# SSD products of a group in one cluster over two banks; transposes of values and x written pairwise

## The chip, the cores and the metric

The kernel runs on one core of a Trainium2 chip. The metric is device microseconds of one execution, the median of several runs; lower is better. A profile is one execution recorded instruction by instruction on the same kind of chip. Engines: PE multiplies matrices, DVE, ACT and POOL work on elements, SP issues most of the transfers.

## The reference

Two residual layers over 272 tokens (16 learned meta tokens and 256 real ones) of width 2048, each a mixer, a projection back and a layer norm. The first mixes with gated linear attention (GLA, 4 heads) and stick-breaking attention (8 heads). The second is a Mamba-2 SSD mixer: 64 heads of width 64 in 8 groups, which share B and C of state size 128 within a group. Without the chunking, what the second layer computes per head is

```python
x, B, C, dt = split(silu(causal_conv(h @ w_in)))
L[t, s]  = exp(sum of dt*a over s < r <= t) for s <= t, else 0
y[t]     = sum_s  (C[t] . B[s]) * L[t, s] * dt[s] * x[s]  +  d_skip * x[t]
out      = rms_norm_per_group(y * silu(z)) @ w_out
```

and GLA per head is, for the output dimension v, `o[t] = sum_s (q[t] * exp(G[t] - G[s])) . k[s] * v[s]` over s <= t, followed by an RMS norm and a SiLU gate.

## The kernel before

All weights stream through as units of 1 MB (`L0`, `L1` list them in order). A unit's weights are split into a high and a low part of reduced-precision fp32 (`whi` by ACT on L146, `wlo` by DVE or POOL on L147, five buffers each), and each product of it is done as three: high by high, high by low, low by high (L165 to L167 for the projections in, L453 to L455 for the second layer's projection out). An "in" unit is 48 such products of 256 to 274 columns, an "out1" unit 24 of 512 columns. They are called the main products here. Projections accumulate in the PSUM tiles `pj` (four banks).

Between them stands the work of the mixers, in full fp32: PE takes every such product in two passes, except transposes, which take one. These write to the PSUM tiles `po` (two banks) or to the two banks `z0`, `z1` (`zbank()` hands them out in turn). A run of fp32 instructions between two main products is called a set. The mixers are generators; `tick()` advances each by one step after a fixed number of main products. A scheduler then orders every engine's instructions by a simulation of its own, so that a piece can be issued later than it is written, and pieces written together can be drawn apart.

The places that the change touches:

- `to_tokens` turns a value unit of GLA or stick-breaking (128 values by 272 tokens) to tokens on partitions: a copy to `vraw` by ACT, then three transposes (L539 twice, L540 for the last 16 tokens), then four copies out of the bank. GLA has four value units a head, so four such sets.
- `mix_gla` multiplies scores by values: for each of four j a bank, three products in parts like the main ones, then the fp32 products of the second token block (L646) and of the last 16 tokens (L647, 16 rows deep).
- Second layer, per group g: units B, C, x0 to x3, z0 to z3, then, from group 2, four out1 units of group g-2. `x_path(g, j)` takes x units two at a time: SiLU (DVE, three ACT steps, a POOL product on L955), then four transposes of 128 columns (L1053) and two of 16 (L1054), then DVE products by dt into `xd` (L1062) and `xd2` (L1064).
- `decay1` makes the matrices `M` of the eight heads (DVE L992 and L993, exp by ACT), the small `mt` for the last 16 tokens, multiplies B by C (L1006 to L1008, in a z bank), masks the result on POOL, and multiplies M (L1019, two of four on POOL from group 2) and mt (L1022) by it.
- `mix_ssd` waits for all of that, then, for each j of four, a bank with two heads side by side in 64 columns each of the PE: first 128 tokens (L1100, 256 columns), second block (L1102, 144 columns), last 16 tokens (L1104, 16 rows deep, 16 columns). After each j: DVE adds the skip term from the bank (L1107), POOL gates (L1108), ACT and DVE write the parts `yh`, `yl`, and the squares are summed, whose sum over partitions (L1123) gives the norm `rr`. That is needed by the out1 units two groups later.

Of the kernel before, what the change touches and what calls it, by code (L numbers as in the profile page):

```python
# [6 lines left out]
F32 = mybir.dt.float32  # L7
# [5 lines left out]
P = 128  # L13
D = 2048
KT = 16
NM = 16
# [72 lines left out]
class _Body:  # L89
# [440 lines left out]

    def to_tokens(self, ps, v0h, v0l, vt1, vt2, j):

        nc = self.nc
        raw = self.lp.tile([P, T], F32, tag="vraw", name=self.nm("vraw"), bufs=2)
        nc.scalar.activation(raw, ps[:, :T], AF.Copy)
        yield
        pt = self.po()
        for t in range(2):
            nc.tensor.transpose(pt[:, t * P : (t + 1) * P], raw[:, t * P : (t + 1) * P], self.ident)  # L539
        nc.tensor.transpose(pt[:16, 256:384], raw[:, 256:272], self.ident)  # L540
        yield
        c = slice(j * P, (j + 1) * P)
        nc.scalar.activation(v0h[:, c], pt[:, :P], AF.Copy)
        nc.vector.tensor_tensor(v0l[:, c], pt[:, :P], v0h[:, c].bitcast(F32), op=ALU.subtract)
        nc.scalar.activation(vt1[:, c], pt[:, P : 2 * P], AF.Copy)
        nc.vector.tensor_copy(vt2[:, c], pt[:16, 256:384])

    def post_gv(self, ps, h, j):
        lp = self.lp
        if j == 0:  # L550
            self.cur["v", h] = (
                lp.tile([P, 512], F32R, tag="gv0h", name=self.nm("gv0h"), bufs=2),
                lp.tile([P, 512], F32R, tag="gv0l", name=self.nm("gv0l"), bufs=2),
                lp.tile([P, 512], F32, tag="gvt1", name=self.nm("gvt1"), bufs=2),
                lp.tile([16, 512], F32, tag="gvt2", name=self.nm("gvt2"), bufs=2),
            )
            self.tasks["gate", h] = self.push(self.gate_gla(h))
        self.tasks["v", h, j] = self.push(self.to_tokens(ps, *self.cur["v", h], j))

# [54 lines left out]
    def mix_gla(self, h):  # L614
# [4 lines left out]
        g = self.cur["r", h]  # L619
        yield from _wait(self.tasks["r", h], *[self.tasks["v", h, j] for j in range(4)])  # L620

# [16 lines left out]
        u = lp.tile([P, 4, T], F32, tag="gu", name=self.nm("gu"))  # L638
        sq = lp.tile([P, T], F32, tag="gsq", name=self.nm("gsq"))
        for j in range(4):  # L640
            o = self.po()
            c = slice(j * P, (j + 1) * P)
            mm(o[:, :T], v0h[:, c], sh, start=True, stop=False, skip_group_check=True)
            mm(o[:, :T], v0h[:, c], sl, start=False, stop=False, skip_group_check=True)
            mm(o[:, :T], v0l[:, c], sh, start=False, stop=False, skip_group_check=True)
            mm(o[:, 128:T], vt1[:, c], s[:, 288:432], start=False, stop=False, skip_group_check=True)  # L646
            mm(o[:, 256:T], vt2[:, c], s[:16, 0:16], start=False, stop=True, skip_group_check=True)  # L647
            vec.tensor_tensor(u[:, j, :], o[:, :T], g[:, j, :], op=ALU.mult)
# [38 lines left out]
    def post_sv(self, ps, h, j):  # L687
# [6 lines left out]
        )  # L694
        t = self.push(self.to_tokens(ps, *v, 0))
        self.mixers[4 + h // 4].append(self.push(self.mix_sb(h, self.cur["q"], self.cur["k"], v, t)))
# [276 lines left out]
    def decay1(self, g):  # L973
# [42 lines left out]
        for h in range(0, HPG, 2):  # L1016
# [3 lines left out]
            yield  # L1020
        c = cb[:16, 0:16].rearrange("p (o c) -> p o c", o=1).broadcast_to([16, HPG, 16])
        vec.tensor_tensor(mt, mt, c, op=ALU.mult)  # L1022
        yield

    def post_x(self, ps, g, j):
        lp = self.lp
        if j == 0:
            self.cur["x", g] = lp.tile([P, 4, T], F32, tag="xts", name=self.nm("xt"), bufs=2)
            self.cur["xd", g] = (
                lp.tile([P, 2, 512], F32, tag="xd", name=self.nm("xd")),  # L1030
                lp.tile([16, 512], F32, tag="xd2", name=self.nm("xd2")),
            )
        xt = self.cur["x", g]
# [4 lines left out]
    def x_path(self, g, j):  # L1038
        nc, vec = self.nc, self.nc.vector
        xt = self.cur["x", g]  # L1040
        xd, xd2 = self.cur["xd", g]
# [7 lines left out]
        pt = self.po()  # L1049
        p2 = self.po()  # L1050
        for i in range(2):
            for t in range(2):
                nc.tensor.transpose(pt[:, t * 256 + i * P : t * 256 + (i + 1) * P], xt[:, j + i, t * P : (t + 1) * P], self.ident)  # L1053
            nc.tensor.transpose(p2[:16, i * P : (i + 1) * P], xt[:, j + i, 256:T], self.ident)  # L1054
        yield
        h0 = g * HPG + 2 * j
        c = slice(j * P, j * P + 256)
        hv = lambda a: a.rearrange("p (h c) -> p h c", c=64)
        bd = lambda a: a.rearrange("p (h o) -> p h o", o=1)
        for t in range(2):  # L1060
            d = bd(self.est[:, 1, t, h0 : h0 + 4]).broadcast_to([P, 4, 64])
            vec.tensor_tensor(hv(xd[:, t, c]), hv(pt[:, t * 256 : (t + 1) * 256]), d, op=ALU.mult)  # L1062
        d = bd(self.est2[:, 1, h0 : h0 + 4]).broadcast_to([16, 4, 64])
        vec.tensor_tensor(hv(xd2[:, c]), hv(p2[:16, :256]), d, op=ALU.mult)  # L1064
        yield
# [19 lines left out]
    def mix_ssd(self, g):  # L1085
        nc, lp = self.nc, self.lp
        act, vec, mm = nc.scalar.activation, nc.vector, nc.tensor.matmul
        M, xt, z = self.cur["M", g], self.cur["x", g], self.cur["z", g]
        xd, xd2 = self.cur["xd", g]
        yield from _wait(self.tasks["decay", g], *[self.tasks[a, g, j] for a in "xz" for j in (1, 3)])  # L1090
        yh, yl = self.mix[g] = self.y_tiles() if g else self.y0
        sq = lp.tile([P, S], F32, tag="ysq", name=self.nm("ysq"))
        for j in range(4):
            o = self.po()
            c = [slice(j * P + i * 64, j * P + (i + 1) * 64) for i in range(2)]
            r = [o[i * 64 : (i + 1) * 64, :] for i in range(2)]
            h = [2 * j, 2 * j + 1]
            gk = dict(skip_group_check=True)
            for i in range(2):
                mm(r[i][:, 0:S], xd[:, 0, c[i]], M[:, h[i], 0:256], start=True, stop=False, **gk)  # L1100
            for i in range(2):
                mm(r[i][:, 112:S], xd[:, 1, c[i]], M[:, h[i], 256:400], start=False, stop=False, **gk)  # L1102
            for i in range(2):
                mm(r[i][:, 240:S], xd2[:, c[i]], self.mt[:, h[i], :], start=False, stop=True, **gk)  # L1104
            yield
            u = lp.tile([P, S], F32, tag="yu", name=self.nm("yu"), bufs=2)
            vec.scalar_tensor_tensor(u, xt[:, j, NM:T], self.col(C_DS, 4 * g + j), o[:, :S], op0=ALU.mult, op1=ALU.add)  # L1107
            nc.gpsimd.tensor_tensor(u, u, z[:, j, :], op=ALU.mult)  # L1108
# [142 lines left out]
```

## Time and profile before

| | |
|---|---|
| median of 3 runs | 1430.6 us (1430.48 to 1431.33) |
| profiled execution | 1430.63 us, span of its instructions 1428.9 us |
| PE busy | 1408.6 us, 99% of the span |
| DVE, ACT, POOL busy | 980.7, 762.7, 334.0 us |
| DMA | 249.83 MB, mean 175 GB/s |

In the views, a line names the line of the kernel, the engine, the operation, what is written and read (buffer numbers left out), the shape and the count. A timeline row begins with the start and the duration in us; neighbouring instructions that are alike are merged into one row with a count. Matmuls are pipelined: a main product of 256 columns is shown as lasting 0.28 us, but they start 0.11 to 0.12 us apart, so the cost on PE is read from the starts. PEclk is the clock that PE was granted, 1.00 being full.

### The profile page before, as it was taken

The numbers are of one execution on the slowest core, as the hardware profiler recorded it, in microseconds if no ns is written. First come the engines' busy times: TensorE is split into PE (matmuls) and PEld (weight loads), VectorE is DVE, ScalarE is ACT, GpSimd is POOL, SyncE is SP. The second block draws the span as 40 slices with busy tenths as digits, with TensorE's granted clock in tenths as the row PEclk, the third lists the DMA queues.
The fourth block names the chain that finished last, engine by engine and source line by source line (L and its number), as shares of the span: only waits on it lengthen the run. The fifth ranks groups of instructions, "written<-read, shape, count | busy, mean of one in ns | idle before, by whom it ended". The sixth has DMA issues, their size and how long they took to land. (4 is left out here: it accounts for less than half of the span.)

```text
span 1428.9 us, 26055 instructions
## 1 busy us (share of the span) xinstructions
PE 1408.6 (99%) x10780; PEld 1337.7 (94%) x10780; DVE 980.7 (69%) x1522; ACT 762.7 (53%) x1133; POOL 334.0 (23%) x287
## 2 busy tenths in 40 slices
PE   9999999999999999999999999999999999999996
PEld 8999999999999999999999999899898998989985
DVE  6746574575565465447799989576876767767677
ACT  6545454354344544445587656565555555555651
POOL 0000100100101010004401535343432433434323
PEclk9999999999999999999999999999999999999998
DMA  8545444445454445444435554564554555445651
GB/s 318 181 151 173 153 153 172 167 159 177 148 178 148 148 148 192 148 148 144 150 132 216 193 199 166 207 225 167 206 178 166 207 181 220 153 172 179 207 207 59
DMA packets 37719, 249.83 MB, mean 175 GB/s; under 512 B 4256, under 2 KB 6112, under 8 KB 9184
## 3 DMA queue, kind: packets, MB, share of 16 engines
q1 hardware_dynamic: 37168, 247.77, 49.5%
q8 instruction: 84, 1.38, 0.4%
q10 hardware_dynamic: 432, 0.39, 0.1%
q14 instruction: 35, 0.29, 0.1%
HBM read 245.94 MB, written 2.20 MB: 174 GB/s over the span
## 5 line engine op out<-in xcount | busy, mean ns | idle before, releaser
L165 PE MATMUL pj<-xhi,whi 128*128 128x272 f32 (+4 forms) x2560 | 733.7, 287 | 1.8 <-DVE fix L845 1.5
L166 PE MATMUL pj<-xlo,whi 128*128 128x272 f32 (+4 forms) x2560 | 731.1, 286 | 0.1
L167 PE MATMUL pj<-xhi,wlo 128*128 128x272 f32 (+4 forms) x2560 | 730.2, 286 | 0.0
L147 DVE TENSOR_TENSOR wlo<-raw,whi 128x1024 fp32r<-128x1024 f32 (+2 forms) x405 | 508.9, 1260 | 280.7 <-ACT whi L146 278.3
L146 ACT ACTIVATE whi<-raw 128x1024 fp32r<-128x1024 f32 (+2 forms) x435 | 451.1, 1039 | 393.0 <-PE pj L166 324.8
L165 PEld LDWEIGHTS pj<-xhi,whi 128*128 128x128 f32 x2560 | 481.6, 188 | 5.1 <-DVE fix L845 1.9
L166 PEld LDWEIGHTS pj<-xlo,whi 128*128 128x128 f32 x2560 | 482.3, 188 | 2.1 <-issue 0.6
L167 PEld LDWEIGHTS pj<-xhi,wlo 128*128 128x128 f32 x2560 | 481.7, 188 | 0.5
L165 PE MATMUL pj<-mixh,whi 128*128 128x272 f32 x384 | 111.6, 292 | 0.0
L166 PE MATMUL pj<-mixl,whi 128*128 128x272 f32 x384 | 110.5, 288 | 0.0
L167 PE MATMUL pj<-mixh,wlo 128*128 128x272 f32 x384 | 110.2, 287 | 0.0
L147 POOL TENSOR_TENSOR wlo<-raw,whi 128x1024 fp32r<-128x1024 f32 x30 | 75.6, 2521 | 134.7 <-ACT whi L146 129.5
L453 PE MATMUL pj<-whi,yh 128*128 128x512 f32 (+1 forms) x244 | 97.3, 399 | 0.0
L454 PE MATMUL pj<-wlo,yh 128*128 128x512 f32 (+1 forms) x244 | 94.9, 389 | 0.0
L455 PE MATMUL pj<-whi,yl 128*128 128x512 f32 (+1 forms) x244 | 94.3, 386 | 0.0
L248 POOL TENSOR_TENSOR gr<-gr,gsc 128x1088 f32<-128x1088 f32 x6 | 15.4, 2572 | 307.0 <-ACT gsc L247 307.0
L165 PEld LDWEIGHTS pj<-mixh,whi 128*128 128x128 f32 x384 | 72.1, 188 | 0.5
L166 PEld LDWEIGHTS pj<-mixl,whi 128*128 128x128 f32 x384 | 72.3, 188 | 0.3
L167 PEld LDWEIGHTS pj<-mixh,wlo 128*128 128x128 f32 x384 | 72.3, 188 | 0.1
L462 DVE SCALAR_TENSOR_TENSOR acc<-pj,rr,acc 128x512 f32<-128x512 f32 (+1 forms) x65 | 47.4, 737 | 28.3 <-PE pj L455 28.2
L1108 POOL TENSOR_TENSOR yu<-yu,gz 128x256 f32<-128x256 f32 x32 | 44.9, 1408 | 82.2 <-DVE yu L1107 79.1
L455 PEld LDWEIGHTS pj<-whi,yl 128*128 128x128 f32 x244 | 45.9, 188 | 9.8
(309 smaller groups left out, 1497.8 us busy)
## 6 DMA issues: line engine op xcount, KB each, us to landing
raw<-in_wts SPq DMA_DIRECT2D x212, 1024.0 KB, 4.8
ebc<-edr SPq DMA_DIRECT2D x8, 1664.0 KB, 6.5
raw<-in_wts SPq DMA_DIRECT2D x9, 256.0 KB, 5.4
hacc<-in_xT SPq DMA_DIRECT2D x7, 272.0 KB, 5.4
early<-in_wts SPq DMA_DIRECT2D x2, 512.0 KB, 7.5
lg<-in_lnr SPq DMA_DIRECT2D x1, 1024.0 KB, 4.6
lb<-in_lnr SPq DMA_DIRECT2D x1, 1024.0 KB, 5.9
out_h<-acc SPq DMA_DIRECT2D x2, 512.0 KB, 2.6
```

Source lines behind the costliest of these rows:

```text
L146: self.nc.scalar.activation(hi, src, AF.Copy)
L147: eng.tensor_tensor(lo, src, hi.bitcast(F32), op=ALU.subtract)
L165: mm(ps, whi, xhi, start=first, stop=False)
L166: mm(ps, whi, xlo, start=False, stop=False)
L167: mm(ps, wlo, xhi, start=False, stop=last)
L248: mul(c, c, e, op=ALU.mult)
L453: mm(ps, yh[:, kk, tt], hi[:, k, :], start=kk == 0, stop=False)
L454: mm(ps, yh[:, kk, tt], lo[:, k, :], start=False, stop=False)
L455: mm(ps, yl[:, kk, tt], hi[:, k, :], start=False, stop=kk == 3)
L462: self.nc.vector.scalar_tensor_tensor(a, ps, r[:, t : t + 1], a, op0=ALU.mult, op1=ALU.add)
L1108: nc.gpsimd.tensor_tensor(u, u, z[:, j, :], op=ALU.mult)
```

## The change

1. SSD. The products of a group's eight heads are written together: two banks `po`, four heads in each (two pairs of heads, one after the other along the bank's 512 columns). Per bank the first-block products of both pairs, then the second-block products of both (now L1135 for both), then the last 16 tokens.
2. The last 16 tokens of two heads become one product (L1141): `mt2` and `xd2` hold one head's 16 tokens on partitions 0 to 15 and another's on 32 to 47, with zeros in the rest, so a product is 48 rows deep and 32 columns wide. There are four a group where there were eight. The two tiles are cleared once at the second layer's start (two DVE instructions), and filled by four DVE instructions each (L1043, L1093) where mt took one and xd2 two.
3. x. `x_path` for the first two x units only does the SiLU. That of the last two transposes all four: into both `po` banks (L1074), the 16-token pieces into a z bank (L1078).
4. GLA. Two value units are turned by one `to_tokens` (now L538, L539), with the copy to `vraw` made at once behind the unit; and the products of two j stand together in the text, so that L655 and L656 (before L646, L647) of both follow one another.

The scheduler's order of PE's instructions shows what becomes of this. First the SSD products of group 3, PE, before: the set of the first of four j, among the products of an out1 unit (M, mt, xd as above).

```order
L454 MATMUL pj_11351<-wlo_11292,yh_9659 128x512
L455 MATMUL pj_11351<-whi_11291,yl_9660 128x512
L1100 MATMUL po_11377<-M_10806,xd_10851 64x256 x2
L1102 MATMUL po_11377<-M_10806,xd_10851 64x144 x2
L1104 MATMUL po_11377<-mt,xd_1370_10852 64x16 x2
L453 MATMUL pj_11350<-whi_11319,yh_9659 128x512
L454 MATMUL pj_11350<-wlo_11320,yh_9659 128x512
```

The same place now:

```order
L454 MATMUL pj_11345<-wlo_11286,yh_9661 128x512
L455 MATMUL pj_11345<-whi_11285,yl_9662 128x512
L1135 MATMUL po_11371<-M_10798,xd_10843 64x256 x4
L1135 MATMUL po_11371<-M_10798,xd_10843 64x144 x4
L1141 MATMUL po_11371<-mt_7920,xd_7921 64x2x16 x2
L1135 MATMUL po_11372<-M_10798,xd_10843 64x256 x4
L1135 MATMUL po_11372<-M_10798,xd_10843 64x144 x4
L1141 MATMUL po_11372<-mt_7920,xd_7921 64x2x16 x2
L453 MATMUL pj_11344<-whi_11313,yh_9661 128x512
```

Four sets, each 12 main products behind the one before, have become one; so it is in groups 1 to 7. In group 0 the scheduler draws the products into four sets.

Second, the transposes of x0 and x1 in the same group, PE, before: they stand 21 products into unit z0, the bank `pj_11086` in these rows.

```order
L167 MATMUL pj_11086<-xhi,wlo_11021 128x256
L1053 MATMUL po_11005<-ident,xt_10850 128x128 x2
L1054 MATMUL po_11006<-ident,xt_10850 16x128
L1053 MATMUL po_11005<-ident,xt_10850 128x128 x2
L1054 MATMUL po_11006<-ident,xt_10850 16x128
L165 MATMUL pj_11086<-xhi,whi_11020 128x256
```

Now they stand at the end of z0 (`pj_11069`), ahead of z1 (`pj_11150`).

```order
L167 MATMUL pj_11069<-xhi,wlo_11036 128x256
L1074 MATMUL po_11132<-ident,xt_10842 128x128 x4
L1078 MATMUL z_64<-ident,xt_10842 16x128 x2
L165 MATMUL pj_11150<-xhi,whi_11070 128x256
L166 MATMUL pj_11150<-xlo,whi_11070 128x256
```

The transposes of x2 and x3 do not join them: they remain a set of their own, 1 product into z2 (before, 9 products into z2). So it is in every group: 16 sets of x transposes before and 16 now. In groups 3 to 7 the first set moves back by 11 to 36 products, the second forward by 1 to 30.

Third, the transposes of two value units of GLA's head 2, PE, before: each pair of units has such a set in one unit after the other; here the first.

```order
L165 MATMUL pj_2344<-xhi,whi_2310 128x272
L539 MATMUL po_2389<-ident,vraw_2371 128x128 x2
L540 MATMUL po_2389<-ident,vraw_2371 16x128
L166 MATMUL pj_2344<-xlo,whi_2310 128x272
L167 MATMUL pj_2344<-xhi,wlo_2311 128x272
```

Now both stand in one unit (`pj_2431`), with four main products between them.

```order
L538 MATMUL po_2472<-ident,vraw_2342 128x128 x2
L539 MATMUL po_2472<-ident,vraw_2342 16x128
L165 MATMUL pj_2431<-xhi,whi_2389 128x272
L166 MATMUL pj_2431<-xlo,whi_2389 128x272
L167 MATMUL pj_2431<-xhi,wlo_2390 128x272
L165 MATMUL pj_2431<-xhi,whi_2389 128x272
L538 MATMUL po_2473<-ident,vraw_2427 128x128 x2
L539 MATMUL po_2473<-ident,vraw_2427 16x128
```

They moved nearer to each other, but are still two sets: 24 sets of value transposes before and 24 now. Of GLA's products of scores and values, which were 16 sets, four pairs have joined, and one more set has joined a neighbouring fp32 product.

The diff, cut to its core (`gk` is `skip_group_check`):

```diff
-    def to_tokens(self, ps, v0h, v0l, vt1, vt2, j):
+    def to_tokens(self, raws, v0h, v0l, vt1, vt2, j):
-        raw = self.lp.tile([P, T], F32, tag="vraw", name=self.nm("vraw"), bufs=2)
-        nc.scalar.activation(raw, ps[:, :T], AF.Copy)
         yield
-        pt = self.po()
+        pts = [self.po() for _ in raws]
...
 mix_ssd:
-        for j in range(4):
-            o = self.po()
-            for i in range(2):
-                mm(r[i][:, 0:S], xd[:, 0, c[i]], M[:, h[i], 0:256], start=True, stop=False, **gk)
-            for i in range(2):
-                mm(r[i][:, 112:S], xd[:, 1, c[i]], M[:, h[i], 256:400], start=False, stop=False, **gk)
-            for i in range(2):
-                mm(r[i][:, 240:S], xd2[:, c[i]], self.mt[:, h[i], :], start=False, stop=True, **gk)
-            yield
+                os = [self.po() for _ in range(2)]
+                for p, o in enumerate(os):
+                    o = o.rearrange("p (j t) -> p j t", j=2)
+                    for s, t0, c0, c1 in ((0, 0, 0, 256), (1, 112, 256, 400)):
+                        for jj in range(2):
+                            for i in range(2):
+                                h = 4 * p + 2 * jj + i
+                                mm(o[i * 64 : (i + 1) * 64, jj, t0:S], xd[:, s, h * 64 : (h + 1) * 64], M[:, h, c0:c1],
+                                    start=(s, jj) == (0, 0), stop=False, **gk)
+                    for i in range(2):
+                        n = 2 * p + i
+                        mm(o[i * 64 : (i + 1) * 64, :, 240:S], self.xd2[:, n, :], self.mt2[:, n], start=False, stop=True, **gk)
+                yield
...
 layer1:
+        self.mt2 = lp.tile([48, 4, 2, 16], F32, tag="mt2", name="mt2")
+        self.xd2 = lp.tile([48, 4, 64], F32, tag="xd2", name="xd2")
+        nc.vector.memset(self.mt2, 0.0)
+        nc.vector.memset(self.xd2, 0.0)
 decay1:
-        vec.tensor_tensor(mt, mt, c, op=ALU.mult)
+        for j in range(2):
+            for p in range(2):
+                vec.tensor_tensor(self.mt2[32 * j : 32 * j + 16, 2 * p : 2 * p + 2, j, :], m[:, j, p], c, op=ALU.mult)
 x_path:
+        if j == 0:
+            return
+        pts = [self.po(), self.po()]
+        p2 = self.zbank()
...
```

More of the change, by code (lines that the diff above doesn't have):

```diff
@@ L619, in mix_gla @@
         g = self.cur["r", h]
-        yield from _wait(self.tasks["r", h], *[self.tasks["v", h, j] for j in range(4)])
+        yield from _wait(self.tasks["r", h], *[self.tasks["v", h, j] for j in (1, 3)])
         zb = self.zbank()
@@ L694, in post_sv @@
         )
-        t = self.push(self.to_tokens(ps, *v, 0))
+        raw = lp.tile([P, T], F32, tag="vraw", name=self.nm("vraw"), bufs=2)
+        self.nc.scalar.activation(raw, ps[:, :T], AF.Copy)
+        t = self.push(self.to_tokens([raw], *v, 0))
         self.mixers[4 + h // 4].append(self.push(self.mix_sb(h, self.cur["q"], self.cur["k"], v, t)))
@@ L1028, in post_x @@
             self.cur["x", g] = lp.tile([P, 4, T], F32, tag="xts", name=self.nm("xt"), bufs=2)
[L1029 to L1032, printed above, removed]
+            self.cur["xd", g] = lp.tile([P, 2, 512], F32, tag="xd", name=self.nm("xd"))
         xt = self.cur["x", g]
```

100 lines of the change are left out of this document (63 added, 37 removed).

## The prediction

> **What bounds the kernel.** I read the page's busy times first, then the busy time by stage, then PE's waits, then the timeline of PE around the places that change. On the page, the span, the engines, and the group of the weight splits on ACT:
>
> ```profile
> span 1428.9 us, 26055 instructions
> PE 1408.6 (99%) x10780; PEld 1337.7 (94%) x10780; DVE 980.7 (69%) x1522; ACT 762.7 (53%) x1133; POOL 334.0 (23%) x287
> L146 ACT ACTIVATE whi<-raw 128x1024 fp32r<-128x1024 f32 (+2 forms) x435 | 451.1, 1039 | 393.0 <-PE pj L166 324.8
> ```
>
> PE is busy 1408.6 of 1428.9 us. ACT's splits sat idle 324.8 us until PE freed a buffer for them, so the weights are ahead of PE, not behind. By stage (columns: busy us of PE, weight loads, DVE, ACT, POOL, then granted clock, DMA share, GB/s):
>
> ```profile
> 40.00:700.00 660.00, 660.00 (x5251) 649.82 (x5251) 392.77 (x588) 317.59 (x476) 75.67 (x105) 1.00 0.47 160
> 700.00:760.00 60.00, 56.51 (x439) 54.23 (x438) 53.16 (x115) 45.38 (x85) 0.00 (x0) 1.00 0.44 156
> 865.00:1385.00 520.00, 517.89 (x3789) 473.29 (x3788) 378.47 (x545) 294.19 (x410) 199.65 (x130) 1.00 0.53 189
> ```
>
> The first layer leaves PE no gap, groups 2 to 7 of the second leave it 2.1 us in 520, with DVE at 73% and the clock at 1.00. Only the boundary of the layers (700 to 760) has DVE nearly full. PE's waits (us in total, times, longest):
>
> ```profile
> PE po L1053 <- POOL xt L955: 3.1, 5, 1.2
> PE pj L165 <- DVE fix L845: 1.5, 2, 0.8
> ```
>
> So what leaves PE leaves the time, one for one, unless PE then waits. The sum is against the profiled execution, 1430.63 us (span 1428.9 and 1.7 around it), which is the median of the runs. A measurement here tells about 0.2%, 2.9 us, from no change.
>
> **SSD products, groups 1 to 7.** One set of group 4, PE's timeline:
>
> ```profile
> 1085.71 0.39 PE L454 MATMUL pj<-wlo,yh 128*128 128x512 f32 x1
> 1085.94 0.39 PE L455 MATMUL pj<-whi,yl 128*128 128x512 f32 x1
> 1086.25 0.65 PE L1100 MATMUL po<-M,xd 128*64 128x256 f32 x4
> 1086.74 0.41 PE L1102 MATMUL po<-M,xd 128*64 128x144 f32 x4
> 1087.08 0.29 PE L1104 MATMUL po<-mt,xd 16*64 16x16 f32 x4
> 1087.30 0.50 PE L453 MATMUL pj<-whi,yh 128*128 128x512 f32 x1
> 1087.64 0.40 PE L454 MATMUL pj<-wlo,yh 128*128 128x512 f32 x1
> ...
> 1088.59 0.39 PE L455 MATMUL pj<-whi,yl 128*128 128x512 f32 x1
> ```
>
> Two main products start 0.23 us apart (1085.71 to 1085.94). From 1085.94 to 1087.64 are 1.70 us where two such steps would take 0.46 less rounding (0.455): the set costs 1.25. Of it 0.09 is entry (1085.94 + 0.23 = 1086.17, the set starts at 1086.25), 0.11 exit (1087.30 to 1087.64 is 0.34 for 0.23), and 1.05 the set itself. A group has four: 5.0 us. What the pieces cost when they follow each other, group 0 shows, where two sets once stood together without L1104:
>
> ```profile
> 797.73 0.65 PE L1100 MATMUL po<-M,xd 128*64 128x256 f32 x4
> 798.21 0.41 PE L1102 MATMUL po<-M,xd 128*64 128x144 f32 x4
> 798.45 0.60 PE L1100 MATMUL po<-M,xd 128*64 128x256 f32 x4
> 798.88 0.41 PE L1102 MATMUL po<-M,xd 128*64 128x144 f32 x4
> ...
> 805.02 0.41 PE L1102 MATMUL po<-M,xd 128*64 128x144 f32 x4
> 805.36 0.29 PE L1104 MATMUL po<-mt,xd 16*64 16x16 f32 x4
> 805.58 0.65 PE L1100 MATMUL po<-M,xd 128*64 128x256 f32 x4
> ```
>
> L1100 takes 0.48 behind something else and 0.43 behind the same kind; L1102 0.24, but 0.34 where the 16 rows follow (805.02 to 805.36); L1104 0.22 (805.36 to 805.58), also with L1100 behind it. A bank of the new set is 0.48 + 0.43 + 0.24 + 0.34 + 0.22 = 1.71. Two banks with one entry and exit are 3.62. The product of 48 rows and 32 columns is in no row; its bounds are L1104's 0.22 a pair and twice that, 0.44. Since even L1102's 144 columns go in 0.24, I take 0.24: 3.65 a group. Saved 5.0 - 3.65 = 1.35, in seven groups 9.5 us; by the upper end (3.62 + 0.44) 6.6. If 48 rows need no change like that to 16 rows (0.34 for 0.24, 0.10 a bank), 0.2 a group is saved besides, 1.4 in all, and the term is 10.9. I stay with 9.5, since the only row with fewer than 128 rows shows the change.
>
> The Trainium skill ("TensorEngine Tiling", Key Properties) says that PE drains when its tiling mode changes, not when the tile does, and lists a 64-row mode beside the 32-row one. The trace agrees with the 0.10 at L1104; no row here has 48 rows. By that rule 48 rows pay as 16 do, 9.5, and the 10.9 would be out.
>
> **Group 0** had its products in three sets and has them in four, spread over 60 main products: one entry and exit more (0.20), four pairs of small products fewer. Between 0 and 1.35, I take 0.5. **After a set** the next four main products start 0.95 us apart in all (1087.64 to 1088.59) where 0.91 is normal; 21 sets in groups 1 to 7 are gone, 0.04 each: 0.9.
>
> **GLA's products.** Five joins each save an exit. Of the next rows, the second follows 0.24 us behind the first where 0.12 to 0.13 is normal, since the first comes behind fp32: 0.11, in all 0.5 us.
>
> ```profile
> 175.02 0.40 PE L644 MATMUL po<-s0l,gv0h 128*128 128x272 f32 x1
> 175.26 0.28 PE L645 MATMUL po<-s0h,gv0l 128*128 128x272 f32 x1
> ```
>
> **Transposes.** The order keeps 24 sets of value transposes and 16 of x; the count of instructions is the same, so by themselves they save 0. What moves is when PE meets them. The first x set of most groups waits for POOL's SiLU product; in group 5:
>
> ```profile
> 1151.38 0.28 PE L165 MATMUL pj<-xhi,whi 128*128 128x256 f32 x1
> 1152.45 0.44 PE L1053 MATMUL po<-ident,xt 128*128 128x128 f32 x2 [0.80 <-POOL xt L955]
> ```
>
> Here 1.07 us lie where 0.11 is normal, 0.96 lost for the 0.80 that the row calls idle. The waits row has 3.1 in five such waits, 1.2 of it in group 1. For groups 2 to 7 that is 1.9, with some 0.16 more for each of four, and a few shorter ones: 3.0. The first set now comes 11 to 36 products later, 1.3 to 4.1 us at 0.115, and these waits go. But the second set now comes earlier. In group 4, unit x3 ends where z0 starts, at 1060.00, and POOL's product for x2 and x3 ends at 1074.11:
>
> ```profile
> 1060.00 0.28 PE L165 MATMUL pj<-xhi,whi 128*128 128x256 f32 x1
> 1070.38 2.40 POOL L147 TENSOR_TENSOR wlo<-raw,whi 128x1024 fp32r<-128x1024 f32 x1 [8.81 <-ACT whi L146]
> 1072.74 1.37 POOL L955 TENSOR_TENSOR xt<-xt,xcl 128x544 f32<-128x544 f32 x1
> ```
>
> That is 14.1 us. The changed order puts the second set 105 main products (9 into z2) and the first set of about 0.65 behind that point: 105 x 0.115 + 0.65 = 12.7. So up to 1.4 us of new wait a group, or none where POOL's split of 2.40 no longer stands ahead (in group 4 it now stands behind). Between 0 and 8 us for six groups I take 2.0, nearer to none, because in the trace of before this set mostly came without a wait. Net 1.0 saved.
>
> **DVE and the rest.** Two clearings at the layers' boundary, where DVE is full: the nearest row has 0.28 us for 272 columns, so 128 and 256 columns take some 0.4 together, and I count them whole, 0.4 lost. The four products into mt2 and four into xd2 a group, for one and two, lie beside PE: DVE has 27% free in groups 2 to 7, and the splits that queue behind them are ahead of PE by the row of L146. If that cover went, a late wlo would stop PE. The M of the next group can be written once the last product has read the old one, so it is now made in one stretch ahead of the adds of the out1 unit (L462), which free `pj`; 16 instructions of about 0.24 us are 3.8, while PE has a whole unit of 24 products (5.5 us) and a half one before it needs that bank: hidden. SP has the same transfers, the decay's a little earlier; POOL's four gating products come closer together, with nothing on PE waiting for them for over 150 main products.
>
> ```profile
> 764.77 0.28 DVE L919 MEMSET dt_scr<- 64x272 f32 x1
> L1022 DVE TENSOR_TENSOR mt<-mt,cb x8: 268/1998/2006, 797.2 to 1317.3; 16x128 f32<-16x128 f32 x8
> ```
>
> **The sum**: 9.5 + 0.5 + 0.9 + 0.5 + 1.0 - 0.4 = 12.0 us; 1430.6 - 12.0 = 1418.6.
>
> **Rivals.** *The cheaper case*: the row change falls away (1.4 more), the second x sets do not wait (2.0), and the boundary's 1.5 us of waits for `fix` do not return, since the order there has changed: 12.0 + 4.9, 1413.7. For it: second sets came without a wait in most groups. Against: DVE at the boundary has 53 us of work in 60.
>
> *The waits come back*: every second x set of six groups waits 1.3 us, 7.8 instead of 2.0, and nothing is left for group 0: 12.0 - 5.8 - 0.5 = 5.7 saved, 1424.9. For it: the scheduler placed the first sets before, too, where it thought POOL done, and they waited.
>
> *The other side: DVE held by POOL.* The row of L1022 above shows the small product into mt at 268 ns once undisturbed, but 1998 in the median: it runs beside POOL's products into M, 2.7 us each, and ends with them. There are now four such instructions a group. If each is held so, DVE loses 3 x 2.0 = 6 us more a group, right where splits queue; if half of that reached PE, seven groups lose 21 us: 1430.6 - 12.0 + 21 = 1439.6. It decides from 1.7 us a group on PE (12.0 / 7). Against it: PE had no wait for wlo at all, with 2 us already lost there in each of six groups. The Trainium skill speaks for this one ("SBUF — State Buffer", section "two separate sides"): a DVE instruction with two SBUF inputs and one of GpSimd shut each other out for the whole instruction, which the 1998 ns agree with; the first of the four would then wait, and the others as often as POOL starts anew.
>
> *It does nothing*: if sets cost what their passes cost wherever they stand, entry, exit and the small products would be paid elsewhere: 1429 to 1431. Against: the entry and exit are in the rows, 0.20 a set, and three a group are gone from the order.
>
> **Chances.** The sum 0.70 (own range 1414.5 to 1422.5), the cheaper case 0.13, the waits 0.09, DVE held 0.04, nothing 0.04. The first three are faster by over 0.2%: 0.92; nothing is within 0.2%: 0.04; DVE held is slower: 0.04. The range runs from below the cheaper case to beyond the returning waits, 1412.5 to 1425.5, which leaves out the last two.
>
> **What the profile after would show.** L1135 and L1141 in one set a group of 3.6 to 3.7 us between main products, in groups 1 to 7; the pair L1141 at 0.22 to 0.26; no wait at the first x set, and waits of L1074 for POOL under 2 us in all at the second; wlo never waited for by PE. The prediction is wrong if L1141 costs 0.4 or more, if PE waits for L955, for `fix` or for M by more than 5 us, or if a wait for wlo or L462 appears in groups 2 to 7.

## The result: 9.6 us faster

The changed kernel takes 1420.94 us (median of 4 runs, 1420.52 to 1421.82), the kernel before 1430.54 beside it: a ratio of 0.9933, 95% interval [0.9916, 0.995]. The prediction of 1418.6 (range 1412.5 to 1425.5) holds, 2.3 us too low. The page after, its first lines and the splits' group:

```profile
span 1418.8 us, 25974 instructions
PE 1398.8 (99%) x10716; PEld 1339.0 (94%) x10716; DVE 999.0 (70%) x1564; ACT 762.0 (54%) x1133; POOL 322.5 (23%) x287
L146 ACT ACTIVATE whi<-raw 128x1024 fp32r<-128x1024 f32 (+2 forms) x435 | 451.5, 1040 | 395.8 <-PE pj L166 328.4
```

The span fell by 10.1 us. PE has 64 products fewer and 9.8 us less busy time, DVE 18 us more: PE is still what everything stands behind. By stage, the boundary of the layers, groups 0 and 1, and groups 2 to 7 (columns as before):

```profile
700.00:760.00 60.00, 56.98 (x447) 54.95 (x445) 53.91 (x117) 45.57 (x85) 0.00 (x0) 1.00 0.45 157
760.00:865.00 105.00, 102.01 (x857) 97.68 (x857) 97.51 (x190) 70.27 (x111) 35.26 (x31) 1.00 0.60 217
865.00:1385.00 520.00, 519.18 (x3773) 482.17 (x3772) 404.53 (x582) 300.17 (x415) 192.48 (x132) 1.00 0.54 190
```

One SSD set, group 4, in PE's timeline:

```profile
1081.67 0.39 PE L454 MATMUL pj<-wlo,yh 128*128 128x512 f32 x1
1081.89 0.39 PE L455 MATMUL pj<-whi,yl 128*128 128x512 f32 x1
1082.21 1.57 PE L1135 MATMUL po<-M,xd 128*64 128x256 f32 x16
1083.71 0.30 PE L1141 MATMUL po<-mt,xd 48*64 48x32 f32 x4
1083.95 1.57 PE L1135 MATMUL po<-M,xd 128*64 128x256 f32 x16
1085.45 0.30 PE L1141 MATMUL po<-mt,xd 48*64 48x32 f32 x4
1085.69 0.50 PE L453 MATMUL pj<-whi,yh 128*128 128x512 f32 x1
1086.03 0.39 PE L454 MATMUL pj<-wlo,yh 128*128 128x512 f32 x1
```

From 1081.89 to 1086.03 are 4.14 us where two steps between main products are 0.455: the set costs 3.68, as it does in all seven groups (3.677 to 3.681), and L1141 takes 0.24 (1083.71 to 1083.95). Before, four sets of 1.25 stood there. PE's waits, whole kernel:

```profile
PE po L1135 <- DVE xd L1087: 1.8, 2, 1.0
PE po L905 <- ACT acc L906: 1.2, 1, 1.2
PE po L1161 <- POOL ysq L1155: 1.2, 1, 1.2
PE po L1074 <- POOL xt L973: 0.7, 2, 0.5
PE pj L165 <- DVE fix L863: 0.3, 1, 0.3
```

The first row is new and all in group 0. The x transposes still wait a little (0.7, against 3.1 before). The wait for `fix` is nearly gone, and the one for `acc` has grown from 0.5.

### The profile page after: what moved, and what is told of

It is laid out like the page before. It is cut to its first block, busy times and chain, and to the rows that moved or that the text cites. A ratio compares the mean times of both kernels' runs of the same rounds, so it can differ in the third digit from the quotient of the medians.

```text
span 1418.8 us, 25974 instructions
## 1 busy us (share of the span) xinstructions
PE 1398.8 (99%) x10716; PEld 1339.0 (94%) x10716; DVE 999.0 (70%) x1564; ACT 762.0 (54%) x1133; POOL 322.5 (23%) x287
## 4 chain that ended last, share of the span: by engine, by line
PE 84%; DVE 6%; ACT 3%; issue 2%; POOL 2%; DMA 2%; SPq 0%; ACTq 0%; POOLq 0%; DVEq 0%
PE pj L165 22%; PE pj L167 21%; PE pj L166 21%; PE pj L453 4%; PE pj L454 4%; PE pj L455 4%; DVE wlo L147 2%; PE po L1135 1%; ACT whi L146 1%; DVE xlo L779 1%; POOL wlo L147 1%; DMA ebc<-edr 1%; ACT hacc L892 1%; POOL xt L973 1%; DVE xt L962 1%
## 5 line engine op out<-in xcount | busy, mean ns | idle before, releaser
L462 DVE SCALAR_TENSOR_TENSOR acc<-pj,rr,acc 128x512 f32<-128x512 f32 (+1 forms) x65 | 46.2, 735 | 15.2 <-PE pj L455 15.1
L453 PEld LDWEIGHTS pj<-whi,yh 128*128 128x128 f32 x244 | 45.8, 188 | 9.1
```

The source lines that it names most:

```text
L453: mm(ps, yh[:, kk, tt], hi[:, k, :], start=kk == 0, stop=False)
L462: self.nc.vector.scalar_tensor_tensor(a, ps, r[:, t : t + 1], a, op0=ALU.mult, op1=ALU.add)
```

## The experiments

Each kernel was timed in five rounds beside the kernel before on the same chip. The times of all of them (ratio with its 95% interval):

| kernel | us, median | ratio to before |
|---|---|---|
| the whole change | 1420.94 | 0.9933 [0.9916, 0.995] |
| e1 SSD cluster alone | 1429.74 | 0.9989 [0.9981, 0.9998] |
| e2 without the GLA pairs | 1421.42 | 0.9929 [0.9917, 0.9942] |
| e3 x transposes alone | 1428.72 | 0.998 [0.9971, 0.9989] |
| e4 last tokens head by head | 1421.33 | 0.9927 [0.9915, 0.9939] |
| e5 SSD cluster alone, mt2 on POOL | 1420.46 | 0.9926 [0.9914, 0.9939] |
| e6 x transposes two, one, two, one | 1419.61 | 0.9919 [0.9906, 0.9933] |
| e7 fewer rows last | 1418.37 | 0.9911 [0.9898, 0.9925] |
| e8 e6 and mt2 on POOL | 1417.53 | 0.9904 [0.9888, 0.9919] |
| e9 e8 and e7 | 1417.16 | 0.9893 [0.9878, 0.9908] |
| e10 e9, clearings on POOL | 1416.63 | 0.9892 [0.9879, 0.9906] |
| e11 before, mt on POOL | 1428.94 | 0.998 [0.997, 0.9989] |
| e12 e10, x transposes early | 1417.89 | 0.9902 [0.9888, 0.9916] |

The kernel before had medians of 1431.36, 1431.24 and 1431.46 us beside e1 to e4, e5 to e8 and e9 to e12. So ratios are what can be compared across these, to about 0.0015 (2 us). Smaller effects are read from the traces.

### e1: the SSD cluster alone

The kernel before with `mix_ssd`, `mt2` and `xd2` of the changed one; in `x_path` of before only the last product differs:

```diff
-        d = bd(self.est2[:, 1, h0 : h0 + 4]).broadcast_to([16, 4, 64])
-        vec.tensor_tensor(hv(xd2[:, c]), hv(p2[:16, :256]), d, op=ALU.mult)
+        for k in range(2):
+            vec.tensor_tensor(self.xd2[32 * k : 32 * k + 16, j : j + 2, :], ...)
```

> The kernel before, with the merged SSD cluster and its 48-row product alone; value and x transposes as before. Theory (sets cost by entry, exit and pieces): the seven SSD sets of groups 1 to 7 cost 3.68 us each as in the changed kernel, 9.3 less than 28 sets of 1.25; the products of group 0 stand in one set here instead of three, 0.8 less; the five waits of the x transposes for POOL (3.1 us) stay. 10.1 saved: 1420.5 us, as fast as the whole change. Rival (the x transposes carry a good part of the change's 9.6 us): 1423.5 or more. Rival (group 0 waits for xd wherever it stands merged): 1422. Main products of 256 columns keep the before's 114.7 ns if the 4-and-2 order of the x transposes set them to 117.8.

Measured: 1429.74 us. By its number the first rival holds, but not by its reason: the sets cost what they should (3.68 us each, in group 0 too as one set, with a wait), and yet only 1.6 us came out. PE's waits in this kernel say where the rest is:

```profile
PE po L1059 <- POOL xt L961: 8.0, 6, 2.2
PE z L1012 <- POOL bc L961: 2.6, 1, 2.6
PE po L1113 <- DVE xd L1068: 1.2, 1, 1.2
```

The x transposes wait 8.0 us instead of 3.1. Counted by the distance of the products' starts, the first x sets of groups 2 to 7 lose 9.0 us, before 2.6. The worst stands in group 4, where a step between main products is 0.11 us:

```profile
1061.25 0.28 PE L167 MATMUL pj<-xhi,wlo 128*128 128x256 f32 x1
1063.75 0.44 PE L1059 MATMUL po<-ident,xt 128*128 128x128 f32 x2 [2.22 <-POOL xt L961]
```

What made x late there stands on DVE and POOL ahead of it. DVE and then POOL of e1 in group 4:

```profile
1053.30 4.55 DVE L1031 TENSOR_TENSOR mt<-mt,cb 16x32 f32<-16x32 f32 x4
1057.88 0.44 DVE L957 TENSOR_SCALAR xcl<-xt 128x544 f32<-128x544 f32 x1
...
1052.48 2.67 POOL L1025 TENSOR_TENSOR M<-M,cb 128x800 f32<-128x800 f32 x1
1055.12 2.39 POOL L147 TENSOR_TENSOR wlo<-raw,whi 128x1024 fp32r<-128x1024 f32 x1
1061.43 2.27 POOL L961 TENSOR_TENSOR xt<-xt,xcl 128x544 f32<-128x544 f32 x1 [3.92 <-DVE xt L950]
```

The same place in the kernel before, DVE alone:

```profile
1054.33 2.00 DVE L1022 TENSOR_TENSOR mt<-mt,cb 16x128 f32<-16x128 f32 x1
1056.26 0.42 DVE L951 TENSOR_SCALAR xcl<-xt 128x544 f32<-128x544 f32 x1
```

Four products of 32 columns, 0.18 us each when undisturbed, take 4.55 us: the first ends when POOL's product into M ends (1055.15), the second when POOL's split ends (1057.51). The clamp of SiLU queues behind them, 1.6 us later than before; POOL's product into x then takes 2.27 us, beside DVE's splits, where it took 1.37. That is the rival "DVE held by POOL", with one or two of the four held, not all. The second is held only in groups 4 and 7, where a split follows POOL's product into M at once. In groups 2, 3, 5 and 6 only the first is held, 1.9 us, hardly different from the one product before (2.0). Of the 6.4 us that the first sets lose more than before, 3.8 are in groups 4 and 7; the rest is not taken apart. The Trainium skill's rule ("SBUF — State Buffer", section "two separate sides") says this: a DVE instruction with two SBUF inputs and one of GpSimd shut each other out for a whole instruction. The rows agree (1.90 and 2.42 us for the two that are held, 0.18 for the others).

The two longest waits cost more than themselves. Behind each, 2.58 us for `bc` in group 1 and 2.22 for x in group 4, the granted clock falls to 0.50 for 3.41 us, and main products of 256 columns start 0.213 us apart. The second of these stretches (columns as before):

```profile
1064.90:1068.30 3.40, 3.40 (x18) 3.40 (x17) 3.32 (x8) 1.05 (x1) 0.00 (x0) 0.50 0.51 214
```

By an estimate from these numbers the two stretches cost 3.4 us.

### e2: without the GLA pairs

The rest is as changed; `post_gv` and `mix_gla` go back as `to_tokens` does:

```diff
-    def to_tokens(self, raws, v0h, v0l, vt1, vt2, j):
+    def to_tokens(self, ps, v0h, v0l, vt1, vt2, j):
...
-        pts = [self.po() for _ in raws]
+        pt = self.po()
```

> The whole change but the pairing of the value transposes and of the GLA products, which are as before. Theory (the paired sets were kept apart or pay for the change of rows instead of the exit): 1421 us, as the whole change, within 0.4; the GLA sets and value transposes cost the same in total, 15.4 us or so for both kernels. Rival (five joins save 0.11 us each, as the prediction had it): 0.5 slower than the whole change, 1421.5.

Measured: 1421.42 us, the whole change within what can be told; the time alone cannot tell the theory from the rival's 0.5 us. The traces can: 16 sets of GLA's products cost 12.25 us together (0.766 each). In the changed kernel a pair costs 1.526, twice a single one (0.764), and the 24 sets of value transposes cost 8.00 us before and 8.03 after. This part of the change did nothing on PE.

### e3: the x transposes alone

The kernel before with the changed `x_path`; `xd2` stays one tile of 16 rows, written at once:

```diff
+        d = bd(self.est2[:, 1, g * HPG : (g + 1) * HPG]).broadcast_to([16, HPG, 64])
+        vec.tensor_tensor(hv(xd2), hv(p2[:16, :]), d, op=ALU.mult)
```

> The kernel before, with the x transposes alone turned later, both sets after unit x3, four 128-row products and then two 16-row ones; SSD products as before. Theory: 3.3 us of waits and set time gone as in the changed kernel, against 1.6 us for main products of 256 columns at 117.8 ns instead of 113.3: 1.7 saved, 1428.8 us. Rival (the pitch comes from the SSD cluster, not from the x sets): 3.3 saved, 1427.2. Rival (the second set waits instead): 1430.5.

Measured: 1428.72 us. That is 2.6 us under the kernel before by the medians of its call, between the theory's 1.7 and the rival's 3.3, so the time does not decide; the pitch does, and speaks for the theory. All 16 sets cost 0.66 us but one (0.92), 10.8 together, where they were 15.6 with their waits. The main products of 256 columns went from 114.7 to 116.7 ns, without the SSD cluster.

The parts do not add up. e1 and e3 save 1.6 and 2.6 us by the medians of their call (1431.36 for the kernel before), together 4.3, and the whole change saves 9.6. The cluster makes x late, and moving the transposes hides it. In group 4 of the changed kernel DVE is held just as long, but the set stands further on:

```profile
1049.97 4.55 DVE L1043 TENSOR_TENSOR mt<-mt,cb 16x32 f32<-16x32 f32 x4
1058.10 2.30 POOL L973 TENSOR_TENSOR xt<-xt,xcl 128x544 f32<-128x544 f32 x1 [3.92 <-DVE xt L962]
...
1060.98 0.28 PE L167 MATMUL pj<-xhi,wlo 128*128 128x256 f32 x1
1061.10 0.60 PE L1074 MATMUL po<-ident,xt 128*128 128x128 f32 x4
```

POOL's product into x ends at 1060.40 and the set starts at 1061.10, without a wait.

### e4: the last tokens head by head

```diff
-                    for i in range(2):
-                        n = 2 * p + i
-                        mm(o[i * 64 : (i + 1) * 64, :, 240:S], self.xd2[:, n, :], self.mt2[:, n], ...)
+                    for jj in range(2):
+                        for i in range(2):
+                            h = 4 * p + 2 * jj + i
+                            mm(o[i * 64 : (i + 1) * 64, jj, 240:S], xd2[:, h * 64 : (h + 1) * 64], self.mt[:, h, :], ...)
```

`mt` and `xd2` have 16 rows again, so DVE has one product into each, not four, and there is nothing to clear.

> The whole change, but the last 16 tokens head by head: eight products of 16 rows and 16 columns a group in the same cluster instead of four of 48 rows and 32 columns. Theory: a second pair of 16-row products right behind the first costs some 0.1 us a bank (two passes of two small products), 0.2 a group, 1.5 us in all: 1422.4 us. Rival (each pair costs the 0.22 us of the row of the kernel before): 0.44 a group, 3 us in all, 1424. Rival (the small products hide one another): as the whole change, 1421. One set of groups 1 to 7 tells it: 3.68 us in the whole change, 3.9, 4.1 or 3.7 here.

Measured: 1421.33 us. One set, PE's timeline:

```profile
1081.04 1.57 PE L1125 MATMUL po<-M,xd 128*64 128x256 f32 x16
1082.55 0.41 PE L1132 MATMUL po<-mt,xd 16*64 16x16 f32 x8
1082.88 1.57 PE L1125 MATMUL po<-M,xd 128*64 128x256 f32 x16
```

L1132 takes 0.33 instead of 0.24 a bank and a set 3.88 instead of 3.68: the theory's 0.2 a group, 1.4 us in seven. It is not in the time. In the trace other places give it back: the x sets cost 10.6 us instead of 12.3, and group 0's pieces 4.5 instead of 6.2. Against that stand a wait for `bc` (1.2) and the waits for `fix` of before (1.5). So 48-row products buy PE 1.4 us, and about as much is lost elsewhere. That DVE's four products in place of one are the reason is likely, but this run changes the clearings with them.

### e5: the SSD cluster alone, mt2 on POOL

e1 with one word changed:

```diff
-                vec.tensor_tensor(self.mt2[32 * j : 32 * j + 16, 2 * p : 2 * p + 2, j, :], m[:, j, p], c, op=ALU.mult)
+                nc.gpsimd.tensor_tensor(self.mt2[32 * j : 32 * j + 16, 2 * p : 2 * p + 2, j, :], m[:, j, p], c, op=ALU.mult)
```

> The SSD cluster alone again, but the four products into mt2 run on POOL instead of DVE, behind POOL's own products into M. In the first run of the cluster alone (1429.7 us) the first x sets of groups 2 to 7 waited 9.0 us, against 2.6 before. Theory (DVE's four products into mt2 are held by POOL's products into M, 1.9 and 2.4 us for the first two, and DVE's clamp for SiLU queues behind them, so x comes late): the first x sets wait 3 us or less, some 6 us come back, 1423.5 us. Rival (PE is simply earlier by 1.3 us a group and runs into POOL's SiLU product): the waits stay at 8 to 9 us, 1429.5.

Measured: 1420.46 us, 0.0063 under e1 by the ratios, some 9 us, and as fast as the whole change. PE's waits for x, and then DVE and POOL at the same place in group 4:

```profile
PE po L1059 <- POOL xt L961: 2.5, 5, 0.8
```

```profile
1049.33 2.15 DVE L957 TENSOR_SCALAR xcl<-xt 128x544 f32<-128x544 f32 x1
...
1048.52 2.67 POOL L1025 TENSOR_TENSOR M<-M,cb 128x800 f32<-128x800 f32 x1
1051.14 1.17 POOL L1031 TENSOR_TENSOR mt<-mt,cb 16x32 f32<-16x32 f32 x4
```

The clamp now follows M at once; it is held itself (2.15 for 0.42) by the same product of POOL, but not by a second one. The first x sets of groups 2 to 7 lose 2.8 us instead of 9.0. That the two instructions exclude each other is what the rows show; that this cost e1 its gain is shown by the time of e5. The gain is larger than the 6 us expected: the waits for `bc` (2.6 to 1.4) and for `xd` in group 0 (1.2 to 0.3) fell as well, and the two stretches at half the clock are gone, by the estimate above 3.4 us. So some third of the 9 us is the clock, and not the waits themselves. The other runs agree: the mean clock of e1 is 0.993 to 0.996, that of e5 0.996 to 0.998.

### e6: the x transposes in the order of before

```diff
+                k = jj + i
+                nc.tensor.transpose(p2[:16, k * P : (k + 1) * P], xt[:, k, 256:T], self.ident)
-        for i in range(4):
-            nc.tensor.transpose(p2[:16, i * P : (i + 1) * P], xt[:, i, 256:T], self.ident)
```

> The whole change, with the x transposes of a set in the order of before: two products of 128 rows out, one of 16, two, one, instead of four and then two. Everything else stands in the same order. Theory (the order four and two leaves the main products of 256 columns behind it at 117.8 ns instead of 113.3): the products of the units z in groups 1 to 7 go from 116 to 113.5 ns, 28 units of 48, 3.3 us less: 1417.6 us. Rival (the pitch hangs on something else): 116 ns stay, 1421.

Measured: 1419.61 us, a ratio 0.0014 under that of the whole change, which the intervals do not separate. The products of units z in groups 1 to 7 go at 115.3 ns instead of 116.0, not at 113.5: the order within a set is not what sets their pace. The theory falls.

### e7: fewer rows last

```diff
                 for p, o in enumerate(os):
...
+                for p, o in enumerate(os):
+                    o = o.rearrange("p (j t) -> p j t", j=2)
                     for i in range(2):
                         n = 2 * p + i
                         mm(o[i * 64 : (i + 1) * 64, :, 240:S], self.xd2[:, n, :], self.mt2[:, n], ...)
```

and the same in `mix_gla`, vt1 of both tiles ahead of vt2 of both.

> The whole change, but within a cluster all products of 128 rows come first and those of fewer rows last: in SSD both banks' L1135, then both banks' L1141; in GLA vt1 of both tiles, then vt2 of both. Theory (PE pays for each change of rows, 0.10 going down and 0.11 coming back): one change down and back is gone in seven SSD sets and four GLA pairs, 0.1 to 0.2 each, 1.1 to 2.2 us in all: 1419.3. Rival (each small product pays for itself wherever it stands): SSD sets stay at 3.68 us and GLA pairs at 1.53, 1421.

Measured: 1418.37 us. A set, PE's timeline:

```profile
1080.41 0.39 PE L455 MATMUL pj<-whi,yl 128*128 128x512 f32 x1
1080.73 2.93 PE L1136 MATMUL po<-M,xd 128*64 128x256 f32 x32
1083.59 0.42 PE L1144 MATMUL po<-mt,xd 48*64 48x32 f32 x8
1083.94 0.50 PE L453 MATMUL pj<-whi,yh 128*128 128x512 f32 x1
```

An SSD set costs 3.41 instead of 3.68 and a GLA pair 1.230 instead of 1.526: one change from 128 rows to fewer and back is worth 0.27 and 0.30 us, in all 3.1. The rule of the Trainium skill ("TensorEngine Tiling (Array Packing)", Key Properties) that PE drains where its tiling mode changes agrees.

### e8: the order of e6, and mt2 on POOL

The diff of e6, and that of e5 again:

```diff
-                vec.tensor_tensor(self.mt2[...], m[:, j, p], c, op=ALU.mult)
+                nc.gpsimd.tensor_tensor(self.mt2[...], m[:, j, p], c, op=ALU.mult)
```

> The whole change with both the x transposes in the order two, one, two, one and the products into mt2 on POOL. Theory: 3.3 us by the pitch and 1.4 us by the waits of the x sets for POOL that the changed kernel has left (0.66, 0.24, 0.32 and 0.25 us in groups 2, 3, 5 and 6): 1416.2 us. Rival (POOL's longer queue makes x as late as DVE's did): as the variant with the order alone, 1417.6. Rival (neither works): 1421.

Measured: 1417.53 us. No x set of groups 2 to 7 waits any more, all 16 cost 10.7 us together, where the changed kernel has 12.3. That is the second term; the first (the pitch) is refuted, 116.0 ns as in the changed kernel.

### e9 and e10: what worked, together

e9 is e8 with the edit of e7; e10 is e9 with the two clearings on POOL:

```diff
-        nc.vector.memset(self.mt2, 0.0)
-        nc.vector.memset(self.xd2, 0.0)
+        nc.gpsimd.memset(self.mt2, 0.0)
+        nc.gpsimd.memset(self.xd2, 0.0)
```

> What worked, together: the whole change, the products into mt2 on POOL, x transposes in the order two, one, two, one, and the products of fewer rows last in the SSD and GLA clusters. Theory (PE's time leaves the span one for one once no x set waits): 1417.5 us of the variant without the last point, less 7 x 0.27 and 4 x 0.30 = 3.1 us: 1414.4. Rival (the products of 256 columns fall into the slower pitch more often and take it back): 1416 to 1417.

> The same with the two clearings of mt2 and xd2 on POOL, which is idle at the layers' boundary, instead of DVE. Theory (the two clearings shift DVE's queue there: they trade two waits for fix, 1.5 us, for one longer wait for acc, 1.2 us against 0.5): 0.5 us more, 1414.9. Rival (the prediction's term, DVE time lost whole): 0.4 less, 1414.0.

Measured: 1417.16 and 1416.63 us; by their ratios 15 us under the kernel before and some 6 under the whole change (0.9892, interval to 0.9906, against 0.9933 from 0.9916). e10 has the lowest median. Against e8, e9 should have gained 3.1. Its sets do cost 3.41 and 1.23, but group 1 has a wait of 2.0 for POOL's `bc` where e8 had 0.6, so 1.6 is left in the trace, and the span shows 1.3. Here too the granted clock falls to 0.50 for 3.41 us behind the wait (from 818.6), which e8 does not have there. The one run of e9 whose mean clock was 0.998 took 1414.62 us, next to the 1414.4 expected; the others, at 0.995 and 0.996, took 1417.07 to 1418.00. The slower pitch, e9's rival, is the same in both (116.0 ns). e10's two waits in place of e9's:

```profile
PE pj L165 <- DVE fix L864: 1.4, 2, 0.8
PE po L906 <- ACT acc L907: 0.5, 1, 0.5
```

In e9 they are 0.3 and 1.2, as in the changed kernel. So the clearings trade one wait for another (1.5 us together in e9, 1.9 in e10), and the times of e9 and e10 cannot be told apart.

### e11: the kernel before, mt on POOL

```diff
-        vec.tensor_tensor(mt, mt, c, op=ALU.mult)
+        nc.gpsimd.tensor_tensor(mt, mt, c, op=ALU.mult)
```

> The kernel before, with the one product into mt on POOL instead of DVE. Theory (DVE's product into mt is held 2.0 us by POOL's products into M and delays x in the kernel before already): the waits of the first x sets of groups 2 to 7, 2.6 us, fall under 1 us: 1428.8 us. Rival (only a second held product makes x late): the waits stay at 2.5 or more, 1430.9.

Measured: 1428.94 us, 2.5 under the kernel before beside it. PE's waits for x fell from 3.1 to 1.3 us, by the distance of the starts in groups 2 to 7 from 2.6 to 1.4. That is not under 1, as the theory had it, but far from the rival's 2.5: one held product made x late in the kernel before as well, for about half of the waits. The rest of the 2.5 is not settled: the SSD sets of group 0 stand in another order there.

### e12: the x transposes early

e10 with the `x_path` of e1, so that each pair of tiles is turned when it is ready:

```diff
-        if j == 0:
-            return
-        pts = [self.po(), self.po()]
-        p2 = self.zbank()
+        pt = self.po()
+        p2 = self.po()
```

> The variant with the clearings on POOL, but with the x transposes where the kernel before has them, the first two tiles right after unit x1. Theory: the products of 256 columns keep 113.5 ns in groups 1 to 7, as in both kernels run with the early x sets, 3.3 us less than at 116; the x sets wait 3.8 us as in the SSD cluster alone with mt2 on POOL: 0.5 us more than the variant it is made from, 1415.4. Rival (the pitch does not hang on where the x sets stand): 1418.5.

Measured: 1417.89 us, 1.3 over e10 by the medians; the intervals of the ratios overlap. The x sets wait 3.7 us again. The products of 256 columns in groups 1 to 7 go at 113.6 ns. One unit of 48 (z3 of group 4), its first product and what follows its last, in e12 and then in the changed kernel:

```profile
1072.82 0.28 PE L165 MATMUL pj<-xhi,whi 128*128 128x256 f32 x1
...
1078.26 0.39 PE L453 MATMUL pj<-whi,yh 128*128 128x512 f32 x1
```

```profile
1073.72 0.28 PE L165 MATMUL pj<-xhi,whi 128*128 128x256 f32 x1
...
1079.38 0.40 PE L453 MATMUL pj<-whi,yh 128*128 128x512 f32 x1
```

5.44 us for 48 products against 5.66. So the pitch goes with the form of `x_path`, not with the order within a set. This form differs from that of e10 in two things, the place of the sets and the banks that a set writes (the 16-token pieces go to a bank `po`, not to a z bank), and no run separates them. The time lies nearer the rival's 1418.5 than the theory's 1415.4, although the theory's pitch came out: by the distance of the starts the x sets cost 6.6 us more than in e10, not 3.8.

## Why the prediction was right, point by point

**The bound.** PE bounded the kernel, and what left PE left the time: the sets of fp32 products cost 10.4 us less by the distances of the products' starts, the steps between main products 0.6 less, and the span fell by 10.1. The total is nearer than its parts: group 0 missed by 2.2 us one way and the x transposes by 2.3 the other, and that these cancel is luck.

**SSD, groups 1 to 7: 9.5 predicted, 9.3 measured** (28 sets with 35.05 us, 7 with 25.76). The price of the 48-row product, the only one that no row had, was 0.24 as taken. The 48 rows pay the change of rows as 16 do: e7 shows the change itself at 0.27 a set.

**Group 0: 0.5 saved predicted, 1.7 lost.** The step that failed is that four pairs of small products were put against one entry and exit, and nothing was put for the products' input. The new order starts them 22 main products behind the second x set and in four pieces, and PE waits for DVE's products into xd:

```profile
787.33 0.65 PE L1135 MATMUL po<-M,xd 128*64 128x256 f32 x4 [0.81 <-DVE xd L1087]
794.52 1.57 PE L1135 MATMUL po<-M,xd 128*64 128x256 f32 x16 [0.99 <-DVE xd L1087]
```

Without these waits the pieces cost 4.4, as much as before (4.5), so the 0.5 was not there either. In e6, where only the order within the x sets differs, the wait is 0.5 and the sum of the group's pieces 4.9; in e8, with mt2 off DVE besides, 0.6 and 5.4. So it does not hang on mt2. It goes with the order within the x sets: 1.8, 1.6 and 1.6 us in the changed kernel, e2 and e7, which have four and two, against 0.5, 0.6 and 0.8 in e6, e8 and e9 and none in e10, which have two, one, two, one. Why is open.

**After a set: 0.9 predicted, 1.3 measured**: the mean distance of 512-column products went from 228.8 to 227.0 ns, over 742 steps. The same count gives 0.9 less for those of 272 columns and 1.6 more for those of 256, which the prediction had not thought of.

**GLA: 0.5 predicted, 0 measured.** The failed step is "five joins each save an exit". The 0.11 of the exit belongs to the change from 16 rows back to 128, not to that from fp32 to main products, so a second set behind the first pays it all the same. e7 takes it away and gains 0.30 a pair.

**The x transposes: 1.0 predicted, 3.3 measured** (15.6 us with waits, now 12.3). The new waits of the second set, 2.0, came to 0.5, in groups 3 and 6; the first set still waits in groups 2 and 5. Two things were mis-sized: the second sets had a wait of 0.5 before as well, so nothing new came, and 1.5 us were gained in groups 0 and 1, which the term left out. In group 1 the first set had a wait of 1.2 and stood in two pieces.

**The clearings: 0.4 lost predicted.** DVE's time did not carry through; e9 and e10 do not differ.

**DVE held by POOL** was given 0.04 and 1439.6 us. The mechanism is there, 4.55 us on DVE in groups 4 and 7, and where it reaches PE it decides: e1 against e5, 9 us with what the clock adds. What the rival had wrong is the size (a second product is held in two groups only, where it had three more in each) and how it reaches PE. No split came late and no `wlo` was waited for; DVE's next instruction was the clamp for x. The argument against it, that PE waited for no `wlo` with 2 us already lost, looked at the wrong consumer: the waits for x that the prediction did count were in part this (e11). The rival did not come out because the same change moved the transposes past it, 11 to 36 products later.

**What the profile was to show**: the set at 3.68 (3.6 to 3.7 predicted) and the pair at 0.24 are right, L1074 waits 0.7 (under 2), no `wlo` and no L462 is waited for in groups 2 to 7. "No wait at the first x set" is wrong in two groups.

What stays open is 0.9 us between the parts counted (11.0) and the span (10.1); some of PE's records are missing, and start and end are not in the count.

## What to carry to other kernels

Merging small fp32 products pays by their entries, exits and changes of rows, so put those of fewer rows last as well: one trip down and back is 0.27 to 0.30 us here. Before a step is cut in several small instructions on DVE, look at what POOL runs beside them: two tiny products cost 4.3 us of DVE's queue where two long ones of POOL followed each other, and what is behind them in the queue is what comes late. Parts of a change are worth something only together where one hides what the other breaks; a run of each part alone shows which. A wait of PE near 2 us costs more than itself here, so look at the granted clock behind it.

## What was not expected of the hardware

Main products of 256 columns go at one of two paces, 113.3 or 117.8 ns from start to start, and the pace changes at a set of fp32 products. In groups 1 to 7 of both kernels and of e1 to e8, 69 sets stood between two triples of main products (whi by xhi, whi by xlo, wlo by xhi) and were reached at the faster pace; 40 of them left the slower one behind. They divide by `x_path`: 39 of 49 where it is the changed one, 1 of 20 where it is that of before (the kernel before, e1, e5). Of the 49, PE had waited ahead of 7, and all of these kept the faster pace; of the other 42, 39 lost it. A set inside a triple, reached at the faster pace, left the slower one behind in 1 of 18 cases, and one reached at the slower pace set the faster again in 13 of 19. It costs up to 3.3 us here (28 units of 48 products, 2.5 ns). e6 and e8 show that the order in the set is not the cause, e12 that the form of `x_path` matters; whether by the place or by the banks, and why, is open. A change of the triple's order was not tried.

The granted clock falls to 0.50 for 3.41 us behind a long wait. Behind the boundary of the layers, PE sat idle four times for 1.9 us or more in these traces (2.58 and 2.22 in e1, 1.97 in e9, 1.92 in e10), and each time this followed; no shorter wait there, the longest 1.79 us, did it. No run changes the length of a wait by itself, so this is an observation.

DVE's instruction with one SBUF input, the clamp, is held as well: 2.15 us for 0.42 in e5, beside POOL's product into M.
